# One of four block sums per pair moved from a DMA add to a VectorE add, in a product made of seven block products

## The chip, the cores and the metric

The kernel runs on one core of a Trainium2 chip. The metric is the device time of one execution in microseconds (us). The median of three executions of the kernel before is 2121.72 us. The engines are named as the profile names them: PE is TensorE (matmuls), DVE is VectorE, ACT is ScalarE, POOL is GpSimd and SP is SyncE; POOL and SP here mostly issue DMAs.

## The reference, cut to what matters

Two transformer blocks run on 512 tokens of width 1024, in float32. The part that the change touches is the second feed-forward layer (SwiGLU) of the first block:

```python
def swiglu(x, w_gu, w_down):
    g, u = jnp.split(x @ w_gu, 2, axis=-1)
    return (jax.nn.silu(g) * u) @ w_down

u = modulate(rmsnorm(h, norm3_g[l]), mod[:, 2, 0], mod[:, 2, 1])
h = h + FFN_RES_WEIGHT * mod[:, 2, 2][:, None, :] * swiglu(u, ffn2_w_gu[l], ffn2_w_down[l])
```

`w_gu` is 1024 x 5632: 2816 gate columns and as many up columns.

## The kernel before

Every float32 matmul is made of three: each operand is split into a high part (ACT copies it to a rounded type, line 131 for weights, tile `whi`) and a low part (DVE subtracts the high part from the operand, line 132, tile `wlo`), and PE adds high x high, high x low and low x high.

The layer's 22 blocks of 128 gate columns (and their 22 up columns) are taken two at a time, so 11 pairs. Pairs 1 and 2 are computed plainly (`eight_pair`). The other nine (`seven_pair`) use a product with seven block products where the plain way takes eight: the pair's weights and the tokens form a 2 x 2 block matrix each, and sums of blocks are multiplied. Here `w11` and `w12` are the upper and lower 512 rows of the pair's 256 gate columns, `w21` and `w22` those of its up columns. Each block is a tile of 128 partitions x 1024 float32 (512 KB).

The weight sums of a pair are made in `Seven.run`, all four by DMAs that POOL issues and that add into their target (`add`, line 584): `s1 += w22`, `w21 += w11`, `s1 += w11`, `s1 += w12`, where `s1` is loaded with the same data as `w21`. The tile `s1` is therefore used three times, each time with one more summand: the product called q5 here takes it after the first sum, q6 after the second of its sums, q3 after the third. A sum may only be added when the split before it has read `s1`, and the next split waits for the sum. In the trace the tiles `w11`, `w21` and `s1` are all named `w_sum`, and `w12` and `w22` lie in a tile `w_raw`: a DMA `w_sum<-w_sum` is `w21 += w11` or `s1 += w11`, a DMA `w_sum<-w_raw` is `s1 += w22` or `s1 += w12`.

The order on the engines comes from the scheduler, which follows the program as far as data allow. ACT, and DVE behind it, split a pair's seven weights in the order q5, q7 (`w21`), p1 (`w11`), q6, p2 (`w12`), q4 (`w22`), q3, and a split may use a buffer (four of them) only when PE has done with the product four splits earlier: q6 follows the q3 of the pair before, p2 the own q5, q4 the own q7, q3 the own p1. Each product is 24 matmuls of 256 columns. On PE they stand in the order q5, q7, p1, q6, the first 10 matmuls of q4, p2, the other 14 of q4, q3. The product p2 is accumulated on the bank `ca` of p1, so it must wait until ACT has copied p1's result out (line 588); this copy stands on ACT behind the high part of q3's split. Engines and queues take their instructions strictly in order.

The pairs and the down projections (`down_tiles`, lines 162 to 164 with `m_hi` and `m_lo`) alternate: two pairs by seven products, down; three, down; three, down; one, down. "First", "second" and "third" pair below are places in such a group; the group of three that starts at 904.55 us serves as the example. POOL's queue also holds `w21 += w11` of pairs that are still to come. The loads (line 562) are issued by SP, from a ring of six `w_sum` tiles and two `w_raw` tiles.

Of the kernel before, what the change touches and what calls it, by code (L numbers as in the profile page):

```python
# [25 lines left out]
def kernel(  # L26
# [7 lines left out]
    nc = tc.nc  # L34
# [13 lines left out]
    def z_bank(shape=(P, S)):  # L48
        return ps.tile(list(shape), F32, tag="z", name="z_ps")
# [32 lines left out]
    with tc.tile_pool(name="stage", bufs=1) as stage:  # L82
# [41 lines left out]
        def split_w(src, hi=None, lo=None):  # L124
            if hi is None:
                shape = [P, src.shape[1], src.shape[2]]
                hi, lo = (
                    wp.tile([P, 8 * P], F32R, tag=tag, name=tag, bufs=4)[
                        :, 0:shape[1] * shape[2]].rearrange("p (k n) -> p k n", n=shape[2])
                    for tag in ("whi", "wlo"))  # L130
            nc.scalar.activation(out=hi, in_=src, func=AF.Copy)  # L131
            nc.vector.tensor_tensor(out=lo, in0=src, in1=hi.bitcast(F32), op=ALU.subtract)  # L132
            return hi, lo
# [271 lines left out]
        for half in range(2):  # L405
# [4 lines left out]
            for kind in range(2):  # L410
                c0 = kind * D + 512 * half
                pr = z_bank()
                for kk in range(2):
                    wa = stage.tile([P, 4, 512], F32, tag="wa", name="wa", bufs=4)
                    nc.sync.dma_start(
                        out=wa, in_=w_ada[0][512 * kk:512 * (kk + 1), c0:c0 + 512].rearrange(
                            "(k p) n -> p k n", p=P))
# [82 lines left out]
    class Seven:  # L500
# [76 lines left out]
        def run(self, weights, upper, lower):  # L577

            w11, w12, w21, w22, s1 = weights

            def add(to, of):
                nc.gpsimd.dma_start(out=to, in_=of, accum_op=ALU.add)

            def copy(acc):
                v = self.ev()
                nc.scalar.activation(out=v, in_=acc, func=AF.Copy)  # L588
                return v

            add(s1, w22)
            add(w21, w11)
            q5 = split_w(s1)
            add(s1, w11)
            cc = z_bank()
            self.times(cc, q5, self.diff(0), True)
            v5 = copy(cc)
            q7 = split_w(w21)
            cd = z_bank()
            self.times(cd, q7, self.diff(2), True)  # L600
            v7 = copy(cd)
            p1 = split_w(w11)
            ca = z_bank()
            self.times(ca, p1, self.plain(0, H1), True)
            v1 = copy(ca)
            q6 = split_w(s1)
            add(s1, w12)
            cb = z_bank()
            self.times(cb, q6, self.diff(1), True)
            nc.vector.tensor_add(out=v1, in0=v1, in1=cb)  # L610
            p2 = split_w(w12)
            self.times(ca, p2, self.plain(HK, H1), False)
            upper(ca, 0)
            nc.vector.tensor_add(out=v5, in0=v5, in1=v1)
            nc.vector.tensor_sub(out=v7, in0=v7, in1=v5)
            q4 = split_w(w22)
            self.times(cd, q4, self.diff(3), False)
            q3 = split_w(s1)
            self.times(cc, q3, self.plain(HK, H2), False)
            nc.vector.tensor_add(out=v5, in0=cc, in1=v1)  # L620
            upper(v5, 1)
            lower(v7, 1)
            nc.vector.tensor_sub(out=v1, in0=cd, in1=v1)
            lower(v1, 0)
# [112 lines left out]
    with ExitStack() as mx:  # L737
# [140 lines left out]
        with tc.tile_pool(name="mrg", bufs=2) as gp:  # L878
# [28 lines left out]
            for j, cols, w in down_tiles(w_out[0], KT):  # L907
                pd = mm_bank()[:, 0:cols.stop - cols.start]
                with behind(nxt, j, cols):
                    proj(pd, w, mg, cols=cols)  # L910
                nc.vector.scalar_tensor_tensor(out=h[j][:, cols], in0=pd, scalar=gate(1, j),
                                               in1=h[j][:, cols], op0=ALU.mult, op1=ALU.add)
# [7 lines left out]
        out=wfg[:, :, 0:16], in_=wi[:, O_F:O_F + 16].rearrange("(k p) n -> p k n", p=P)))  # L920
# [30 lines left out]
    with ExitStack() as mx:  # L951
        with ExitStack() as ax:
# [5 lines left out]
            with tc.tile_pool(name="att2", bufs=2) as ap:  # L958
# [81 lines left out]
                for j in range(KT):  # L1040
                    nc.vector.scalar_tensor_tensor(out=h[j], in0=h[j], scalar=g_fin[:, j:j + 1],
                                                   in1=pb, op0=ALU.mult, op1=ALU.mult)
# [164 lines left out]
            for m in range(NB):  # L1207
# [5 lines left out]
                for q in range(2):  # L1213
# [5 lines left out]
                                        in1=mhalf[:, 0:1], op=ALU.pow)  # L1219
# [21 lines left out]
        with ExitStack() as gx:  # L1241
            agp = gx.enter_context(tc.tile_pool(name="ga2", bufs=8))
            av = []
            with tc.tile_pool(name="gm2", bufs=2) as gp:
# [4 lines left out]
                for q in range(4):  # L1249
                    w = by_feature(load_w(wi[:, 256 * q:256 * (q + 1)], KT, 256))  # L1250
                    for r in range(2):
# [7 lines left out]
                        for n in range(NB):  # L1259
# [4 lines left out]
                                             in1=bsb[:, g:g + 1, :].to_broadcast([P, NB, P]))  # L1264
                        nc.vector.tensor_mul(out=zu, in0=zu,
                                             in1=mixed.rearrange("p n t -> p (n t)"))
# [46 lines left out]
    with tc.tile_pool(name="ffnb", bufs=2) as fp:  # L1313
        wu = w_up_2[0]
        for pi, (f0, f1) in enumerate(parts):
            ms = []
            for f in range(f0, f1):
# [4 lines left out]
                for br in range(2):  # L1322
# [10 lines left out]
                    for k in (1, 2):  # L1333
                        nc.vector.scalar_tensor_tensor(
                            out=y, in0=xp[:, k:k + S],
# [17 lines left out]
    with tc.tile_pool(name="fin", bufs=2) as fp:  # L1353
# [4 lines left out]
            out=gfb, in_=norm_final_g_2.rearrange("(o n) -> o n", o=1).to_broadcast([P, D]))  # L1358
# [3 lines left out]
        for q in range(4):  # L1362
            cs = slice(256 * q, 256 * (q + 1))
            w = by_row(load_w(w_ple_gate_2[0][:, cs], KT, 256), KT, 256)
            for m in range(NB):
# [24 lines left out]
                if q < 3:  # L1390
# [3 lines left out]
                                               in1=sums[:, m:m + 1], op0=ALU.mult, op1=ALU.add)  # L1394
# [66 lines left out]
```

## Time and profile before

| what | value |
|---|---|
| median of 3 executions | 2121.72 us (2117.65 to 2121.92) |
| the profiled execution, its own time | 2116.4 us |
| its span, first to last instruction | 2114.7 us |
| PE busy | 98% |
| DVE busy | 59% |
| ACT busy | 42% |
| POOL busy | 6% |
| the nine pairs by seven products | 831.6 to 1119.9 us |

The busy shares tell which engine has no room (PE), not what a single stage waits for. For that one reads the stage: where PE stops, what ended each stop, and what that engine had waited for in its turn. A row of the timeline gives the start, the duration, the engine, the line, the operation and its tiles, and in brackets how long the engine had been idle before it and what ended that. A matmul's duration overlaps its neighbours', so the pace of PE is read from start to start.

### The profile page before, as it was taken

To read this page: it belongs to the slowest core of one execution; us is meant where nothing else is said; L and a number is where in the kernel's file an instruction comes from. 1 tells how busy PE (TensorE), PEld (TensorE's weight loads), DVE (VectorE), ACT (ScalarE), POOL (GpSimd) and SP (SyncE) were. 2 spreads that over 40 slices of the span, in tenths; PEclk is the share of its full clock that TensorE was granted. 3 is DMA by queue.
4 is the path that set the end of the run, shared out by engine and by line. 5 is a ranking of instruction groups with operands and counts; after the bars stand their busy time and mean duration, and the time that the engine had idled before them with its cause. 6 is when DMAs were issued, how large, how long until landed. Compare 5 with 4: busy or idle time off the path is not lost.

```text
span 2114.7 us, 26551 instructions
## 1 busy us (share of the span) xinstructions
PE 2075.0 (98%) x10450; PEld 1715.8 (81%) x10450; DVE 1240.5 (59%) x2096; ACT 877.8 (42%) x1366; POOL 125.3 (6%) x192
## 2 busy tenths in 40 slices
PE   7999999999999999999999999999999999999998
PEld 5778888888778888998988876667888888888888
DVE  3775655466653356555657586746554566474665
ACT  4322222357653245333435454645233343242444
POOL 1000000000000000110100011102200000000000
PEclk9999999999999999999999999999999999999999
DMA  9766554331222356776643422213323332333332
GB/s 348 225 217 178 180 178 126 94 100 60 60 81 83 104 146 151 175 177 173 163 112 103 110 80 80 80 50 100 120 80 100 100 100 82 99 99 100 90 128 72
DMA packets 293792, 259.42 MB, mean 123 GB/s; under 512 B 7605, under 2 KB 276090, under 8 KB 293412
## 3 DMA queue, kind: packets, MB, share of 16 engines
q1 hardware_dynamic: 285136, 228.68, 35.4%
q0 software_dynamic: 7840, 27.96, 6.2%
q8 instruction: 82, 1.34, 0.3%
q10 hardware_dynamic: 692, 1.09, 0.1%
q14 instruction: 42, 0.34, 0.1%
HBM read 234.60 MB, written 4.23 MB: 113 GB/s over the span
## 4 chain that ended last, share of the span: by engine, by line
PE 48%; DVE 1%; issue 1%; ACT 1%; DMA 0%; POOL 0%; POOLq 0%; ACTq 0%; DVEq 0%
PE mm_ps L162 12%; PE mm_ps L164 12%; PE mm_ps L163 12%; PE mm_ps L175 2%; PE mm_ps L174 2%; PE mm_ps L176 2%; PE po_ps L1145 2%; PE z_ps L1138 1%; PE z_ps L1099 1%; PE z_ps L1101 1%; PE z_ps L541 0%; PE z_ps L548 0%; PE z_ps L546 0%; PE z_ps L1260 0%; DMA w_sum<-w_raw 0%
## 5 line engine op out<-in xcount | busy, mean ns | idle before, releaser
L131 ACT ACTIVATE whi<-w_raw 128x1024 fp32r<-128x1024 f32 (+2 forms) x340 | 347.1, 1024 | 718.5 <-PE mm_ps L163 552.2
L162 PE MATMUL mm_ps<-uh,whi 128*128 128x512 f32 (+1 forms) x1392 | 541.2, 391 | 5.2 <-ACT uh L307 2.0
L163 PE MATMUL mm_ps<-ul,whi 128*128 128x512 f32 x1392 | 542.1, 390 | 0.0
L164 PE MATMUL mm_ps<-uh,wlo 128*128 128x512 f32 x1392 | 541.5, 389 | 0.0
L132 DVE TENSOR_TENSOR wlo<-w_raw,whi 128x1024 fp32r<-128x1024 f32 (+2 forms) x340 | 408.7, 1204 | 168.5 <-ACT whi L131 164.9
L162 PEld LDWEIGHTS mm_ps<-uh,whi 128*128 128x128 f32 x1392 | 261.7, 189 | 61.2 <-ACT uh L307 3.2
L164 PEld LDWEIGHTS mm_ps<-uh,wlo 128*128 128x128 f32 x1392 | 262.6, 189 | 53.6 <-issue 1.6
L163 PEld LDWEIGHTS mm_ps<-ul,whi 128*128 128x128 f32 x1392 | 262.7, 189 | 52.5 <-issue 0.8
L164 PE MATMUL mm_ps<-m_hi,wlo 128*128 128x512 f32 (+1 forms) x560 | 211.6, 378 | 0.0
L162 PE MATMUL mm_ps<-m_hi,whi 128*128 128x512 f32 (+1 forms) x560 | 211.0, 379 | 0.4 <-DVE h L715 0.4
L163 PE MATMUL mm_ps<-m_lo,whi 128*128 128x512 f32 (+1 forms) x560 | 211.1, 377 | 0.0
L162 PEld LDWEIGHTS mm_ps<-m_hi,whi 128*128 128x128 f32 x560 | 105.2, 188 | 20.5 <-issue 0.8
L163 PEld LDWEIGHTS mm_ps<-m_lo,whi 128*128 128x128 f32 x560 | 105.3, 188 | 20.4 <-issue 0.4
L164 PEld LDWEIGHTS mm_ps<-m_hi,wlo 128*128 128x128 f32 x560 | 105.2, 188 | 20.1
L174 PE MATMUL mm_ps<-whi,uh 128*128 128x512 f32 (+1 forms) x288 | 99.9, 350 | 3.7 <-ACT whi L131 1.6
L175 PE MATMUL mm_ps<-wlo,uh 128*128 128x512 f32 (+1 forms) x288 | 98.8, 344 | 0.8 <-DVE wlo L132 0.8
L176 PE MATMUL mm_ps<-whi,ul 128*128 128x512 f32 (+1 forms) x288 | 97.5, 343 | 0.0
L131 ACT ACTIVATE whi<-w_sum 128x1024 fp32r<-128x1024 f32 x45 | 47.7, 1059 | 118.8 <-PE mm_ps L163 40.9
L132 DVE TENSOR_TENSOR wlo<-w_sum,whi 128x1024 fp32r<-128x1024 f32 x45 | 55.1, 1225 | 58.5 <-ACT whi L131 57.1
L200 DVE SCALAR_TENSOR_TENSOR ada_acc<-ada_w,csil,ada_acc 128x256 f32<-128x256 f32 x196 | 87.3, 481 | 1.9
L548 PE MATMUL z_ps<-uth,wlo 128*128 128x256 f32 x288 | 82.0, 285 | 3.1 <-DVE wlo L132 3.1
L541 PE MATMUL z_ps<-uth,whi 128*128 128x256 f32 x288 | 81.8, 284 | 0.5 <-ACT ev L588 0.4
(355 smaller groups left out, 3154.5 us busy)
## 6 DMA issues: line engine op xcount, KB each, us to landing
w_raw<-in_ffn_w_gu_dram SPq DMA_DIRECT2D x70, 512.0 KB, 5.3
ada_w<-in_w_ada_dram SPq DMA_DIRECT2D x28, 1024.0 KB, 5.2
w_raw<-in_w_up_dram SPq DMA_DIRECT2D x44, 512.0 KB, 4.2
w_raw<-in_w_in_dram SPq DMA_DIRECT2D x20, 1024.0 KB, 5.2
w_sum<-in_ffn_w_gu_dram SPq DMA_DIRECT2D x27, 512.0 KB, 4.4
w_raw<-in_ffn_w_down_dram SPq DMA_DIRECT2D x16, 768.0 KB, 4.5
w_raw<-in_w_mix_in_dram SPq DMA_DIRECT2D x24, 512.0 KB, 5.2
w_sum<-w_sum POOLq DMA_DIRECT2D x18, 512.0 KB, 6.8
```

The source lines that it names most:

```text
L131: nc.scalar.activation(out=hi, in_=src, func=AF.Copy)
L132: nc.vector.tensor_tensor(out=lo, in0=src, in1=hi.bitcast(F32), op=ALU.subtract)
L162: nc.tensor.matmul(acc, lhsT=a, rhs=uhi[:, cols], start=k == 0, stop=False)
L163: nc.tensor.matmul(acc, lhsT=a, rhs=ulo[:, cols], start=False, stop=False)
L164: nc.tensor.matmul(acc, lhsT=b, rhs=uhi[:, cols], start=False, stop=k == n - 1)
L174: nc.tensor.matmul(acc, lhsT=a, rhs=wh, start=k == 0, stop=False)
L175: nc.tensor.matmul(acc, lhsT=a, rhs=wl, start=False, stop=False)
L176: nc.tensor.matmul(acc, lhsT=b, rhs=wh, start=False, stop=k == kt - 1)
L200: nc.vector.scalar_tensor_tensor(out=acc[:, q, :], in0=v[:, k, :], scalar=csil[:, k:k + 1], in1=acc[:, q, :], op0=ALU.mult, op1=ALU.add)
L541: i = nc.tensor.matmul(a, lhsT=whi[:, k, rows], rhs=uhi, start=start and first is None, stop=False, skip_group_check=True)
L548: nc.tensor.matmul(a, lhsT=wlo[:, k, rows], rhs=uhi, start=False, stop=last, skip_group_check=True)
L1145: nc.tensor.matmul(po[64 * hd:64 * hd + 64, b * P:S], lhsT=vts[head // 4][:, b, c0:c0 + 64], rhs=pT, start=b == 0, stop=b == NB - 1, skip_ ...
```

## The change

One of the two sums that follow one another on `s1`, the addition of `w11` between q5 and q6, is made by a DVE instruction on the two tiles. The other three sums of each pair stay DMAs.

```diff
             add(s1, w22)
             add(w21, w11)
             q5 = split_w(s1)
-            add(s1, w11)
+            nc.vector.tensor_add(out=s1, in0=s1, in1=w11)
             cc = z_bank()
             self.times(cc, q5, self.diff(0), True)
```

POOL's queue at the second and third pair of the example group and the first of the next (`w_sum_7380`, `_7378`, `_7379` are `s1`, `w11` and `w21` of the second pair, `_7615`, `_7613`, `_7614` of the third, `_8049` and `_8048` `w21` and `w11` of the next group's first):

```order
 L584 DMA w_sum_7615<-w_raw_7616 128x1024
 L584 DMA w_sum_7614<-w_sum_7613 128x1024
-L584 DMA w_sum_7380<-w_sum_7378 128x1024
 L584 DMA w_sum_7380<-w_raw_7381 128x1024
 L584 DMA w_sum_8049<-w_sum_8048 128x1024
-L584 DMA w_sum_7615<-w_sum_7613 128x1024
 L584 DMA w_sum_7615<-w_raw_7616 128x1024
 L584 DMA w_sum_8284<-w_sum_8283 128x1024
```

The two sums with `w11` are gone; the other DMAs keep their order, `w21 += w11` of a later pair ahead of `s1 += w12` of the running one among them.

DVE at the same third pair (line 615 belongs to the pair before; `wlo_7625`, `wlo_7657` and `wlo_7688` are the low parts of q5, q7 and p1):

```order
 L132 TENSOR_TENSOR wlo_7625<-w_sum_7615,whi_7624 128x1024
 L615 TENSOR_TENSOR ev_7450<-ev_7450,ev_7419 128x512
+L594 TENSOR_TENSOR w_sum_7615<-w_sum_7615,w_sum_7613 128x1024
 L132 TENSOR_TENSOR wlo_7657<-w_sum_7614,whi_7656 128x1024
 L132 TENSOR_TENSOR wlo_7688<-w_sum_7613,whi_7687 128x1024
```

The sum stands two places behind the low part of q5 and directly ahead of that of q7. It stands so in every second and third pair; in the first pair of a group of three it comes directly behind q5's low part and ahead of an instruction of line 715 (down projection into `h`). On PE, ACT and SP no instruction changes its place.

## Rows read from the trace of the kernel before

**Rows 1.** The page: the span, and the engines' busy time, share and instructions.
```profile
span 2114.7 us, 26551 instructions
...
PE 2075.0 (98%) x10450; PEld 1715.8 (81%) x10450; DVE 1240.5 (59%) x2096; ACT 877.8 (42%) x1366; POOL 125.3 (6%) x192
```

**Rows 2.** Waits of PE, 780 to 1130 us: total us, times, longest.
```profile
PE z_ps L548 <- DVE wlo L132: 3.1, 4, 0.9
PE z_ps L541 <- ACT ev L588: 2.7, 5, 0.6
```

**Rows 3.** Timeline of PE: first matmuls of pairs, the matmul behind them, two stops.
```profile
904.55 0.28 PE L541 MATMUL z_ps<-uth,whi 128*128 128x256 f32 x1
...
924.70 0.28 PE L541 MATMUL z_ps<-uth,whi 128*128 128x256 f32 x1
...
937.82 0.39 PE L548 MATMUL z_ps<-uth,wlo 128*128 128x256 f32 x1 [0.88 <-DVE wlo L132]
...
939.61 0.39 PE L541 MATMUL z_ps<-uh,whi 128*128 128x256 f32 x1 [0.56 <-ACT ev L588]
...
947.14 0.28 PE L541 MATMUL z_ps<-uth,whi 128*128 128x256 f32 x1
...
971.17 0.40 PE L162 MATMUL mm_ps<-m_hi,whi 128*128 128x512 f32 x1
...
1023.99 0.28 PE L541 MATMUL z_ps<-uth,whi 128*128 128x256 f32 x1
...
1045.20 0.28 PE L541 MATMUL z_ps<-uth,whi 128*128 128x256 f32 x1
...
1067.04 0.40 PE L162 MATMUL mm_ps<-m_hi,whi 128*128 128x512 f32 x1
```

**Rows 4.** Timeline of ACT in the second pair: high parts p1, q6, q4, q3; copy.
```profile
921.90 1.06 ACT L131 ACTIVATE whi<-w_sum 128x1024 fp32r<-128x1024 f32 x1
930.77 1.06 ACT L131 ACTIVATE whi<-w_sum 128x1024 fp32r<-128x1024 f32 x1 [7.81 <-DMA w_sum<-w_sum]
...
934.87 1.04 ACT L131 ACTIVATE whi<-w_raw 128x1024 fp32r<-128x1024 f32 x1
...
938.01 1.06 ACT L131 ACTIVATE whi<-w_sum 128x1024 fp32r<-128x1024 f32 x1 [1.62 <-DMA w_sum<-w_raw]
938.98 0.58 ACT L588 ACTIVATE ev<-z_ps 128x512 f32<-128x512 f32 x1
```

**Rows 5.** Timeline of POOL in the second and third pair.
```profile
921.30 1.77 POOL L584 DMA_DIRECT2D w_sum<-w_sum  x2 [3.06 <-DMA w_sum<-in_ffn_w_gu_dram]
933.38 0.87 POOL L584 DMA_DIRECT2D w_sum<-w_raw  x1 [10.32 <-DVE wlo L132]
945.17 1.77 POOL L584 DMA_DIRECT2D w_sum<-w_sum  x2 [10.92 <-DVE wlo L132]
```

**Rows 6.** Timeline of DVE: a line 715, then the second and third pair.
```profile
896.59 0.75 DVE L715 SCALAR_TENSOR_TENSOR h<-mm_ps,gate,h 128x512 f32<-128x512 f32 x1 [1.99 <-PE mm_ps L164]
...
921.31 1.23 DVE L132 TENSOR_TENSOR wlo<-w_sum,whi 128x1024 fp32r<-128x1024 f32 x1 [1.46 <-ACT whi L131]
...
931.86 1.23 DVE L132 TENSOR_TENSOR wlo<-w_sum,whi 128x1024 fp32r<-128x1024 f32 x1 [5.54 <-ACT whi L131]
933.01 1.29 DVE L694 TENSOR_TENSOR ev<-ev 128x512 f32<-128x512 f32 x2
...
943.76 1.22 DVE L132 TENSOR_TENSOR wlo<-w_sum,whi 128x1024 fp32r<-128x1024 f32 x1 [0.36 <-ACT whi L131]
```

**Rows 7.** All of lines 132 (ns: min, median, max) and 584 (us).
```profile
L132 DVE TENSOR_TENSOR wlo<-w_raw,whi x340: 681/1224/3368, 8.8 to 2081.8; 128x1024 fp32r<-128x1024 f32 x146, 128x768 fp32r<-128x768 f32 x20, 128x512 fp32r<-128x512 f32 x4
L132 DVE TENSOR_TENSOR wlo<-w_sum,whi x45: 1218/1226/1227, 823.3 to 1109.5; 128x1024 fp32r<-128x1024 f32 x45
...
DMA to landing us min/median/max: 4.5/5.1/9.6
```

**Rows 8.** Timeline of SP: the loads of the third pair's `s1` and `w11`.
```profile
898.71 4.45 SPq L562 DMA_DIRECT2D w_sum<-in_ffn_w_gu_dram  x2
```

## The prediction, made before the changed kernel was run

> **What bounds the kernel now.** I read the page first: PE is busy 98% of 2114.7 us [rows 1], so only a stretch in which PE stops can give time back. Next came the list of what PE waits for while the pairs run: two causes belong to the seven products, low parts of weights that come late from DVE (3.1 us) and a copy on ACT (2.7 us) [rows 2]. These idle times understate the loss, because PE also loses pace around a stop, so I measured whole pairs from start to start [rows 3]. The example group's first pair takes 924.70 - 904.55 = 20.15 us, the pace of a product of 24 matmuls being 20.15 / 7 = 2.88 us. The second takes 947.14 - 924.70 = 22.44, the third 971.17 - 947.14 = 24.03. In the next group the second takes 1045.20 - 1023.99 = 21.21 and the third 1067.04 - 1045.20 = 21.84. Against 20.15 that is 2.29 + 3.88 + 1.06 + 1.69 = **8.92 us of stops**, all in second and third pairs of the two groups of three.
>
> Last I followed one stop back. In the second pair PE stops at 937.82 us for the low part of q4, and at 939.61 for the copy that must precede p2 [rows 3]. On ACT, q4's high part was made at 934.87 and the copy at 938.98, both late because ACT stood 7.81 us, until 930.77, in front of q6's high part, waiting for a DMA `w_sum<-w_sum` [rows 4]: it is `s1 += w11`. POOL had issued that DMA late and in company, directly behind the `w21 += w11` of the next pair, which had to wait for its own load until 921.30 [rows 5]. So the chain is: a POOL queue whose first entry waits for a load, two DMA sums at once, q6, everything behind q6 on ACT, PE. In the third pair the same two-fold issue stands at 945.17 [rows 5].
>
> **What is removed: the wait in front of q6.** Without the DMA, q6's high part needs ACT free (921.90 + 1.06 = 922.96, rows 4) and its buffer, which PE gives back with the end of the pair before, 924.70 [rows 3]. So it can run at 924.7 and not at 930.77, 6.1 us earlier. Its low part ends after 1.06 and 1.23 us and about 0.1 between, at 927.1 [rows 4, 7].
>
> What is late next, step by step on the second pair:
> - p2's buffer comes free with q5, 924.70 + 2.88 = 927.6, and q4's with q7, 930.5. q4's low part then ends at about 932.9. PE wants it after four products, at 936.2, so there are 3.3 us to spare.
> - `s1 += w12` stays a DMA. POOL can issue it 0.3 us behind q6's low part (as at 933.38, where that part, from 931.86, ended at 933.09; rows 5, 6), so at 927.4. From issue to the split that uses it there were 938.01 - 933.38 = 4.63 us [rows 4, 5], which gives 932.0. The split of q3 can't start before its buffer is free with p1, at 924.70 + 3 x 2.88 = 933.3. The DMA is no longer waited for.
> - The copy then ends at 933.4 + 1.06 + 0.58 = 935.0. PE wants p2 after q6 and 10 matmuls of q4, at 924.70 + 4 x 2.88 + 1.2 = 937.4: 2.4 us to spare. This is the thinnest cover. With the longest landing of line 584, 9.6 us [rows 7], the DMA would be there at 937.0, the copy done at 938.7 and PE stopped for 1.3 us.
>
> The third pair, which would start 2.29 us earlier, has the same distances. The price of this part is therefore between -8.92 us (all stops go) and, where the last-named stop remains, some microseconds less; I take -8.92, because the usual landing is the row of this very DMA and not the longest of 36.
>
> **What is added: nine DVE sums.** The trace has no sum of two float32 tiles of this size that writes float32; the nearest rows are the 45 low parts of the same tiles, 1.218 to 1.227 us, and the far end is the longest of line 132, 3.368 us [rows 7]. I take 1.23: 11 us of DVE in all. They lie beside PE as long as nobody on PE waits for what is queued behind. Queued behind are the low parts of q7 and p1. In the second pair DVE idles 1.46 us right there, ahead of 921.31, so the sum fits but for a trifle. In the third the idle time is 0.36 us ahead of 943.76 [rows 6], so q7's low part moves back by 0.8 to 0.9 us, to end near 945.9 if ACT is where it was. PE wants q7 one product into the pair, 947.14 + 2.88 = 950.0 in the old trace and 947.7 in the shifted one: 1.8 us left, more if ACT moves forward too. With 3.368 us in place of 1.23 this would turn into a stop of 0.3 us. In the first pairs the sum stands ahead of line 715, where DVE idles 1.99 us for PE [rows 6]. Over the whole span DVE is busy 59% [rows 1]. The sum waits for nothing new: q5's split has already waited for `s1 += w22`, and `w11` has long been loaded (third pair: issued from 898.71 [rows 8], used near 943). I cost it at nothing, with an upper end of 0.3 us for each of the two third pairs.
>
> **What is moved.** POOL loses nine of 36 issues and nothing overtakes. `w21 += w11` of a later pair still stands ahead of `s1 += w12`. For the third pair that entry is issued at 945.17 [rows 5], once its load is there; that load follows the release of the second pair's raw weights, which comes earlier by the 6 us that q6 gains. Nine DMAs of 512 KB fewer share the DMA engines; I count no gain for that.
>
> One rule speaks against a DVE sum beside POOL's DMAs. POOL's issue at 933.38 ran beside the two-input DVE instructions at 933.01 and kept its 0.87 us [rows 5, 6]. The Trainium skill (SBUF — State Buffer, "SBUF: two separate sides") says that DVE and GpSimd share a port pair under an exclusive lock, taken by a DVE instruction with two SBUF inputs against a GpSimd instruction that reads SBUF, and it tells of a software-issued DMA going from about 620 to 3100 ns beside certain DVE instructions. If the sums did this to the issue of `s1 += w12`, its landing would come some 2.5 us later by that page and eat the cover of p2, which is rival A with a larger chance; the trace shows no such lengthening for instructions of the same kind.
>
> **The sum.** Profiled execution: 2114.7 - 8.92 = 2105.8 us of span, or 2116.4 - 8.92 = 2107.5 us. The median of the runs shown is 5.3 us above the profiled execution, so **2121.72 - 8.92 = 2112.8 us** as a median.
>
> **Rivals.**
> - A. The DMA sum that stays, `s1 += w12`, becomes the last. Then the stops in front of p2 remain. For: in all four bad pairs PE has such a stop, and ACT still waited 1.62 us for this DMA [rows 4]. Against: that wait started late only because q6 did. The four stops with the lost pace around them are about 0.8 us each, 3.3 us; gain 5.6, time 2116.1.
> - B. POOL's queue stays the bound in third pairs: `w21 += w11` of the next group waits for its load and holds `s1 += w12` behind it. It decides if that load lands more than 2.4 us behind the low part of the third q6 (near 947.3). For: POOL stood so until 945.17 in the old trace [rows 5]. Against: the load starts earlier now. Third pairs would keep 3.88 + 1.69; gain 3.35, time 2118.4.
> - C. Slower: DVE takes over a wait that POOL had. If `w11` is not there when the sum's turn comes, DVE stands with all low parts behind it. It decides from about 2 to 5 us, the cover of q7. With a wait like ACT's 7.81 [rows 4] each of the five second and third pairs of the three groups would stop for some 4 us: 20 - 8.9 = 11 us slower, 2132.8. Against: the load is issued some 40 us ahead [rows 8].
> - D. The stops pass to something that no row shows, and nothing is won: 2121.7. That the sum stays a DMA is excluded by the order on POOL and DVE.
>
> **How the numbers follow.** Forecast 0.74, A 0.10, B 0.08, C 0.03, D 0.05. The three executions shown differ by 4.3 us, and about 0.2% (4.2 us) is what a measurement of this kernel can tell from no change. Faster by more than that are the forecast, save for a bad draw, and most of A: 0.82. Within it are B, D and the rest of A: 0.14. Slower: 0.04. The range takes the forecast with the profiled execution's level at its lower end, 2107.5, and reaches over A to about B, 2118.
>
> **What would show it.** After the change the second and third pairs should take 20.2 us each from first matmul to first matmul. ACT should no longer wait for `w_sum<-w_sum` in front of q6, and the waits of PE in lines 541 and 548 should be gone. DVE should show nine instructions of line 594 of about 1.23 us. A is shown by PE stops at line 541 behind the copy; B by a late POOL issue in third pairs only; C by idle time of DVE ahead of line 594 that a load ends. I am wrong if the pairs run at 20.2 us and the time hasn't moved: then a later stage has eaten the gain.

## The result and the profile after the change

The changed kernel takes **2108.57 us** (median of four executions, 2108.18 to 2109.99), the kernel before in the same comparison 2120.01 us (four, 2117.65 to 2121.92). The ratio is 0.9948 with a 95% interval of 0.9931 to 0.9965, so 7.4 to 14.6 us were won. The forecast was a gain of 8.92 us (a ratio of 0.9958) and 2112.8 us. A second comparison (five executions against fifteen) gave 2109.21 us against 2118.87 and a ratio of 0.9956 [0.9942, 0.9969], which is 9.3 us.

The page of the profiled execution, which itself took 2108.77 us; it answers to [rows 1]:

```profile
span 2107.0 us, 26536 instructions
...
PE 2074.2 (98%) x10450; PEld 1717.8 (82%) x10450; DVE 1250.9 (59%) x2105; ACT 878.3 (42%) x1366; POOL 115.3 (5%) x183
```

DVE has nine instructions more and POOL nine fewer; no share tells why the span is 7.7 us shorter. The waits of PE between 780 and 1130 us, all that are left (total us, times, longest):

```profile
PE mm_ps L162 <- ACT ev L671: 2.2, 2, 1.6
PE mm_ps L162 <- ACT uh L633: 1.3, 1, 1.3
PE z_ps L291 <- DVE acc L283: 0.4, 1, 0.4
```

The two rows on lines 541 and 548 [rows 2] are gone. The first matmuls of the second and third pairs of both groups of three, and the matmul behind each group, on PE's timeline [rows 3]:

```profile
926.30 0.28 PE L541 MATMUL z_ps<-uth,whi 128*128 128x256 f32 x1
...
946.46 0.28 PE L541 MATMUL z_ps<-uth,whi 128*128 128x256 f32 x1
...
966.62 0.40 PE L162 MATMUL mm_ps<-m_hi,whi 128*128 128x512 f32 x1
...
1019.44 0.28 PE L541 MATMUL z_ps<-uth,whi 128*128 128x256 f32 x1
...
1039.60 0.28 PE L541 MATMUL z_ps<-uth,whi 128*128 128x256 f32 x1
...
1059.76 0.40 PE L162 MATMUL mm_ps<-m_hi,whi 128*128 128x512 f32 x1
```

Each pair now takes 20.16 us, the late ones too, where they took 22.44, 24.03, 21.21 and 21.84. All nine pairs with their down projections ran from 833.16 to 1112.58 us, 279.42 us, against 288.29 us before (831.57 to 1119.86): 8.87 us less. The stage in one row (length, busy us and count of each engine, granted clock, DMA share, GB/s):

```profile
830.00:1120.00 290.00, 290.00 (x1992) 271.06 (x1991) 178.86 (x206) 120.43 (x154) 20.03 (x23) 1.00 0.56 145
```

PE has no idle time left there. What stood in front of q6 is seen on ACT, in the second pair [rows 4]: the high parts of q6, q4 and q3, then the copy.

```profile
926.43 1.06 ACT L131 ACTIVATE whi<-w_sum 128x1024 fp32r<-128x1024 f32 x1 [1.87 <-PE z_ps L546]
...
932.19 1.06 ACT L131 ACTIVATE whi<-w_raw 128x1024 fp32r<-128x1024 f32 x1 [0.29 <-ACT m_hi L651]
...
935.85 1.06 ACT L131 ACTIVATE whi<-w_sum 128x1024 fp32r<-128x1024 f32 x1 [2.12 <-DMA w_sum<-w_raw]
936.81 0.58 ACT L588 ACTIVATE ev<-z_ps 128x512 f32<-128x512 f32 x1
```

q6 is split 0.13 us after the pair's first matmul (926.30), and it was the buffer that PE gave back that released it. Before, it came 6.07 us after that point. q3 still waited for its DMA, 2.12 us. Over 800 to 1120 us ACT waited for the sums made by DMA as follows, in the kernel before and then after:

```profile
ACT whi L131 <- DMA w_sum<-w_sum: 36.2, 5, 9.4
ACT whi L131 <- DMA w_sum<-w_raw: 18.3, 6, 10.3
```

```profile
ACT whi L131 <- DMA w_sum<-w_raw: 5.9, 3, 2.1
```

POOL in the second and third pair [rows 5]: the two-fold issues are gone, and `s1 += w12` goes out right behind q6's low part (which begins at 927.83, in the DVE rows below).

```profile
923.17 0.88 POOL L584 DMA_DIRECT2D w_sum<-w_sum  x1 [3.41 <-DMA w_sum<-in_ffn_w_gu_dram]
929.34 0.87 POOL L584 DMA_DIRECT2D w_sum<-w_raw  x1 [5.29 <-DVE wlo L132]
943.33 0.87 POOL L584 DMA_DIRECT2D w_sum<-w_sum  x1 [13.11 <-DMA w_sum<-in_ffn_w_gu_dram]
949.50 0.87 POOL L584 DMA_DIRECT2D w_sum<-w_raw  x1 [5.30 <-DVE wlo L132]
```

DVE in the second pair [rows 6]: the new sum, q7's low part, q6's low part. Then all nine sums (ns, minimum, median, maximum).

```profile
921.00 1.22 DVE L594 TENSOR_TENSOR w_sum<-w_sum 128x1024 f32<-128x1024 f32 x1
922.91 1.23 DVE L132 TENSOR_TENSOR wlo<-w_sum,whi 128x1024 fp32r<-128x1024 f32 x1 [0.69 <-ACT whi L131]
...
927.83 1.22 DVE L132 TENSOR_TENSOR wlo<-w_sum,whi 128x1024 fp32r<-128x1024 f32 x1
```

```profile
L594 DVE TENSOR_TENSOR w_sum<-w_sum x9: 1219/1220/1228, 824.9 to 1082.5; 128x1024 f32<-128x1024 f32 x9
```

No sum had to wait for data, and q7's low part behind it came after ACT anyway, with 0.69 us to spare.

Why the span fell by 7.7 us and not by 8.87: the pairs began 1.59 us later in this execution, and what follows them was 0.4 us shorter. The later start is already there at 100 us: the copy of line 131 that begins at 100.06 us before begins at 101.87 us after, and at 99.19 us in the second profile of the changed kernel. It goes with the first 75 us, where the granted clock is at its half level (1.2 GHz) for a while in each execution. The stretch from 30 to 75 us before, after, and in the second profile of the changed kernel (the clock is the third number from the end):

```profile
30.00:75.00 45.00, 38.60 (x196) 28.44 (x196) 31.72 (x58) 16.53 (x23) 0.00 (x0) 0.96 0.89 292
```

```profile
30.00:75.00 45.00, 39.23 (x186) 29.06 (x185) 30.42 (x55) 16.23 (x23) 0.00 (x0) 0.89 0.87 284
```

```profile
30.00:75.00 45.00, 39.62 (x202) 29.25 (x199) 32.54 (x59) 16.61 (x24) 0.00 (x0) 0.96 0.92 300
```

In the last of these three the pairs start at 830.45 us, end at 1109.86 (279.41 us again), and the span is 2104.3 us. So the start of the pairs differs between executions of one kernel; the length of the pairs' stage doesn't, and that is what the experiments below are read by. "Stage" means this length.

### The profile page after: what moved, and what is told of

Its sections match the earlier page's. It is cut to its first block, busy times and chain, and to the rows that moved or that the text cites. A ratio compares the mean times of both kernels' runs of the same rounds, so it can differ in the third digit from the quotient of the medians.

```text
span 2107.0 us, 26536 instructions
## 1 busy us (share of the span) xinstructions
PE 2074.2 (98%) x10450; PEld 1717.8 (82%) x10450; DVE 1250.9 (59%) x2105; ACT 878.3 (42%) x1366; POOL 115.3 (5%) x183
## 4 chain that ended last, share of the span: by engine, by line
PE 95%; DVE 2%; ACT 1%; DMA 1%; SPq 1%; issue 1%; POOL 0%; POOLq 0%; ACTq 0%; DVEq 0%
PE mm_ps L162 24%; PE mm_ps L164 24%; PE mm_ps L163 24%; PE z_ps L548 3%; PE z_ps L546 3%; PE z_ps L541 3%; PE mm_ps L174 2%; PE mm_ps L175 2%; PE mm_ps L176 2%; PE po_ps L1145 2%; PE z_ps L822 1%; PE z_ps L1138 1%; PE z_ps L1099 1%; PE po_ps L833 1%; PE z_ps L1101 1%
## 5 line engine op out<-in xcount | busy, mean ns | idle before, releaser
L164 PEld LDWEIGHTS mm_ps<-uh,wlo 128*128 128x128 f32 x1392 | 262.8, 189 | 53.5 <-issue 1.6
L546 PE MATMUL z_ps<-utl,whi 128*128 128x256 f32 x288 | 81.5, 283 | 0.0
```

Source lines behind the costliest of these rows:

```text
L164: nc.tensor.matmul(acc, lhsT=b, rhs=uhi[:, cols], start=False, stop=k == n - 1)
L546: nc.tensor.matmul(a, lhsT=whi[:, k, rows], rhs=ulo, start=False, stop=False, skip_group_check=True)
```

## The experiments

The theory is that of the prediction: the sum `s1 += w11` came late because of where it stood in POOL's queue, this held q6 and all that is behind it on ACT, and PE stopped in the second and third pairs. Its rivals: the DMA as such is too slow, wherever it stands; it is the traffic of nine DMAs more; the gain comes from elsewhere in the nine pairs. Ratios are to the kernel before in the same comparison, with 95% intervals. Diffs are against the changed kernel.

**Second and third pairs only, and the other five only.**

```diff
-            nc.vector.tensor_add(out=s1, in0=s1, in1=w11)
+            if on_dve:
+                nc.vector.tensor_add(out=s1, in0=s1, in1=w11)
+            else:
+                add(s1, w11)
...
-                seven.run(weights, upper, lower)
+                seven.run(weights, upper, lower, f0 in (10, 12, 16, 18))
```

> The DVE sum only in the four second and third pairs of the groups of three; the other five pairs keep the DMA. My theory (PE stopped because q6's split in these four pairs waited for the DMA): all of the gain, every pair 20.2 us from first matmul to first matmul, time 0.4 to 0.55% under the kernel before. Rival (every DMA sum removed gives its share, by less traffic and less work on POOL): 4/9 of the gain, about 0.2%.

Measured: 2109.43 us, 0.9957 [0.9941, 0.9974]; all nine pairs take 20.15 or 20.16 us. The four sums of the late pairs give the whole gain. The other kernel has `f0 in (4, 6, 8, 14, 20)`:

> The complement: the DVE sum only in the first pairs, the second pair of the first group and the last pair; the four late pairs keep the DMA. My theory: no gain, the late pairs at 22.4, 24.0, 21.2 and 21.8 us within 0.5 us each, time within 0.1% of the kernel before. Rival (each sum gives its share): 5/9 of the gain, about 0.28% faster.

Measured: 2119.45 us, 1.0003 [0.9994, 1.0013]; the late pairs take 22.34, 23.79, 22.88 and 22.34 us, and PE's waits of the kernel before are back:

```profile
PE z_ps L548 <- DVE wlo L132: 4.3, 5, 0.9
PE z_ps L541 <- ACT ev L588: 3.1, 6, 0.6
```

Five sums on DVE in pairs that had no stop give nothing. One of the four late pairs missed its expectation: 22.88 us where 21.2 was expected to within 0.5. With it the late pairs lose 10.75 us here and not 8.9, so the size of the stops isn't fixed, though their place is. Where in the nine pairs the gain sits is settled by these two.

**The other sum on DVE.** `w21 += w11` is what stood ahead in the queue. If it goes to DVE, `s1 += w11` stays the DMA it was, with a clear way.

```diff
-            add(w21, w11)
+            nc.vector.tensor_add(out=w21, in0=w21, in1=w11)
             q5 = split_w(s1)
-            nc.vector.tensor_add(out=s1, in0=s1, in1=w11)
+            add(s1, w11)
```

> The other sum goes to DVE: w21 += w11 there, s1 += w11 a DMA as before, so as many DMAs as in the change. Theory that the queue made the wait (the DMA for q6 stood behind a w21 += w11 that waited for its load, and two sums ran at once): the DMA is issued about 0.3 us behind q5's low part, 5 us ahead of the pair's start, lands in 4.6 to 6.5 us, and at most 1.5 us of wait stays in front of q6; pairs 20.2 us, time as the changed kernel within 0.1%. Theory that the latency of a DMA between two uses of s1 is the cost, wherever it is queued: ACT still waits several us in front of q6, late pairs 21 us or more, at most half of the gain.

Measured: 2114.30 us, 0.9982 [0.9972, 0.9991]. The pairs say one thing and the total another. In the pairs the theory holds: all nine take 20.15 to 20.17 us, the stage 279.41 us. POOL, ACT and PE in the second pair (the sum's issue, q6's high part, the pair's first matmul):

```profile
922.63 0.87 POOL L584 DMA_DIRECT2D w_sum<-w_sum  x1 [1.07 <-DVE wlo L132]
```

```profile
929.10 1.06 ACT L131 ACTIVATE whi<-w_sum 128x1024 fp32r<-128x1024 f32 x1 [2.69 <-DVE ev L620]
```

```profile
928.15 0.28 PE L541 MATMUL z_ps<-uth,whi 128*128 128x256 f32 x1
```

The DMA is issued 5.5 us ahead of the pair's start, right when q5's low part is done, and q6 is split 0.95 us into the pair. No stop follows. So the DMA is fast enough when nothing that waits stands ahead of it, and "too slow as such" falls.

Yet the total, expected within 0.1% of the changed kernel, is 5.1 us (0.24%) above its 2109.2. In the profiled executions the loss stands in two places outside the stage. The first is ahead of the pairs. From the first `uh` (line 633) to the first pair's start it takes 835.02 - 781.5 = 53.5 us, in the changed kernel 833.16 - 782.2 = 51.0. Six of the nine sums on DVE wait for loads here, 5.1 us in all. The first does so ahead of the pairs, directly in front of a low part `ul` that PE needs, and PE stops for 0.93 us:

```profile
787.59 1.23 DVE L592 TENSOR_TENSOR w_sum<-w_sum 128x1024 f32<-128x1024 f32 x1 [1.43 <-DMA w_sum<-in_ffn_w_gu_dram]
```

```profile
789.20 0.39 PE L163 MATMUL mm_ps<-ul,whi 128*128 128x256 f32 x1 [0.93 <-DVE ul L636]
```

This is rival C on a small scale, for a sum that the change did not move; the one stop is 0.93 of the 2.5 us, and no row shown here accounts for the rest. The second place is far behind: from the end of the stage to the end of the span it takes 997.0 us, not 994.4. At 1440 us the scheduler has put matmuls in another order, PE stops for 1.88 us at line 174 where the changed kernel stops for 0.76 us, and the granted clock is down behind it:

```profile
1440.00:1444.00 4.00, 2.75 (x7) 2.17 (x8) 4.00 (x5) 2.45 (x5) 0.52 (x1) 0.58 0.17 49
```

The two places make 2.5 + 2.6 = 5.1 us. The two spans differ by 4.4 us, because this execution had reached the first `uh` 0.7 us earlier.

**The last sum on DVE instead.** `s1 += w11` is a DMA again, `s1 += w12` goes to DVE.

```diff
-            nc.vector.tensor_add(out=s1, in0=s1, in1=w11)
+            add(s1, w11)
...
-            add(s1, w12)
+            nc.vector.tensor_add(out=s1, in0=s1, in1=w12)
```

> The other way round: s1 += w12 on DVE, s1 += w11 a DMA as before. Theory (every late split stands behind q6 on ACT): q6 still waits 6 to 9 us, the stops for q4's low part stay (about 1 us in three of the late pairs), only those in front of p2 go (about 0.8 us each): half of the gain or less, 0.1 to 0.25% under the kernel before, late pairs 20.4 to 22.5 us. Rival (any sum taken from POOL's queue relieves it): late pairs at 20.2 us and all of the gain.

Measured: 2111.64 us, 0.9968 [0.9956, 0.9981]. In the groups of three the pairs take 20.15, 22.71, 20.16 and 20.15, 22.92, 20.16 us: second pairs keep their stop, third pairs lose it. POOL, then ACT at q6 of the second pair, then PE's stop in it:

```profile
924.37 1.77 POOL L584 DMA_DIRECT2D w_sum<-w_sum  x2 [3.27 <-DMA w_sum<-in_ffn_w_gu_dram]
945.84 0.87 POOL L584 DMA_DIRECT2D w_sum<-w_sum  x1 [19.70 <-DVE wlo L132]
948.72 0.87 POOL L584 DMA_DIRECT2D w_sum<-w_sum  x1 [2.00 <-DMA w_sum<-in_ffn_w_gu_dram]
```

```profile
933.82 1.06 ACT L131 ACTIVATE whi<-w_sum 128x1024 fp32r<-128x1024 f32 x1 [7.78 <-DMA w_sum<-w_sum]
```

```profile
942.01 0.38 PE L548 MATMUL z_ps<-uth,wlo 128*128 128x256 f32 x1 [2.01 <-DVE wlo L132]
```

In the second pair the two sums still go out together behind a load, and q6 waits 7.78 us, nearly the 7.81 of before. In the third the same DMA goes out alone at 945.84, q6 is split at 951.40, 0.9 us after the pair's first matmul, and there is no stop. It goes out alone because its place in the queue is another: `w21 += w11` of the next group, which stood ahead of it in the kernel before, goes out behind it here, at 948.72, when its load is there. So the company in the queue and the load ahead of it make the stop. The expectation missed this: its theory would have kept a stop in third pairs, with half of the gain or less (0.1 to 0.25%), and the total came out at 0.32%. By the pairs 2.56 + 2.77 = 5.3 of 8.9 us of stops stay, so 3.6 should be won; the total says 6.8 (4.0 to 9.3). The profiled execution is the slowest of the six (2115.49 us). What makes up the rest isn't settled.

**Both sums on DVE.** The changed kernel, and `s1 += w12` by `nc.vector.tensor_add` too.

> The last sum of the chain, s1 += w12, goes to DVE as well. The trace of the changed kernel has no stop of PE left in the pairs, so nothing is to be won: within 0.1% of the changed kernel, and ACT's 2.1 us of waiting in front of q3 gone. Rival (the remaining DMA still costs): up to 0.1% faster. Or DVE now waits for a load: slower, with idle time of DVE in front of the new sum.

Measured: 2107.05 us, 0.9944 [0.9931, 0.9956], with the changed kernel beside it at 0.9956 [0.9942, 0.9969]:

> The changed kernel once more, for a narrower interval. By whole pairs the gain is 8.9 us of some 2120, so a ratio of 0.9958; the first measurement had 0.9948 with 0.9931 to 0.9965. Expected 0.994 to 0.9965.

The intervals overlap, and the medians differ by 0.10%, which theory and rival both allowed; the total can't tell them apart. The pairs can: they take 20.15 or 20.16 us in both, although ACT no longer waits in front of q3 there. The DMA that stayed costs PE nothing, and rival A is excluded from both sides. This kernel isn't shown to be the better one.

**As many DMAs as before.** Each pair adds one block into a buffer in DRAM that nobody reads (it is filled from `h` once, ahead of the pairs), in one kernel in the place of the removed sum, in another at the pair's end.

```diff
             nc.vector.tensor_add(out=s1, in0=s1, in1=w11)
+            nc.gpsimd.dma_start(out=self.ghost, in_=w11, accum_op=ALU.add)
```

> The changed kernel with one more DMA per pair on POOL's queue, which adds w11 into a buffer in DRAM that nobody reads: the number of POOL's DMAs is that of the kernel before, only nobody waits for this one. Theory (the wait in front of q6 was the cost): time as the changed kernel within 0.15%, pairs 20.2 us. Rival (traffic and POOL's work were the cost): late pairs above 21 us again and half of the gain or more lost, 0.2 to 0.5%.

Measured: 2126.37 us, 1.0036 [1.0023, 1.0049], slower than before. It didn't measure traffic, since the scheduler put the added DMA of a later pair ahead of `s1 += w12`, and it waited for that pair's load:

```profile
937.64 0.87 POOL L598 DMA_DIRECT2D ghost<-w_sum  x1 [8.01 <-DMA w_sum<-in_ffn_w_gu_dram]
938.19 1.21 POOL L587 DMA_DIRECT2D w_sum<-w_raw  x1
```

In the changed kernel that sum went out 3.0 us after the pair's first matmul (929.34 - 926.30), here 7.1 us after it (938.19 - 931.05). PE's stops in front of p2 return, in the lines of this kernel:

```profile
PE z_ps L544 <- ACT ev L591: 12.9, 5, 4.2
```

The second pair of the first group takes 26.14 us, the late pairs up to 25.06. It is rival B's mechanism, brought about by the added entry: one DMA that waits for a load, at the head of POOL's queue, costs PE several us. With the added DMA at the end of the pair, behind `s1 += w12`, it stands in nobody's way:

```diff
             q3 = split_w(s1)
+            nc.gpsimd.dma_start(out=self.ghost, in_=s1, accum_op=ALU.add)
```

> The changed kernel with one more DMA per pair on POOL's queue, this time of s1 behind its last sum, so that it stands behind s1 += w12 in the queue and not ahead of it (in the first try the scheduler had put it ahead, with a wait for a later pair's load). It adds into a buffer in DRAM that nobody reads. POOL's issues and the bytes are those of the kernel before. Theory (the wait was the cost): within 0.15% of the changed kernel, pairs 20.2 us. Rival (traffic and POOL's work): late pairs above 21 us, 0.2% or more lost.

Measured: 2110.33 us, 0.9965 [0.9954, 0.9977]. Eight pairs take 20.15 or 20.16 us and one 20.61. POOL issues as many DMAs here as in the kernel before:

```profile
928.38 0.87 POOL L587 DMA_DIRECT2D w_sum<-w_raw  x1 [3.19 <-DVE wlo L132]
935.98 0.87 POOL L622 DMA_DIRECT2D ghost<-w_sum  x1 [6.72 <-DMA w_sum<-w_raw]
```

So neither the number of POOL's DMAs nor their bytes made the 8.9 us (though the added ones write to DRAM); of the stage 0.45 us is lost. Behind the stage the profiled execution lost 1.8 us more, with the granted clock down at 1438 us.

**How much cover DVE has.** Behind the sum, four or eight instructions that put the maximum of `s1` and `s1` into `s1`, each as long as the sum and of no effect on its value.

```diff
             nc.vector.tensor_add(out=s1, in0=s1, in1=w11)
+            for _ in range(4):
+                nc.vector.tensor_tensor(out=s1, in0=s1, in1=s1, op=ALU.max)
```

> The changed kernel with four more DVE instructions of the same size per pair on s1 (the maximum of s1 with itself, in place), 36 in all, 41 to 44 us of DVE time. Theory (DVE has about 5 us of cover ahead of q7 and 4 us ahead of q6 in the pairs): same time as the changed kernel within 0.15%, pairs 20.2 to 20.5 us. Rival (DVE work lies on the path there): up to 44 us, 2% slower.

Measured with four: 2114.82 us, 0.9981 [0.9972, 0.9990]. Thirty-six instructions of 1.22 us, 44 us of DVE, lengthen the stage by 3.2 us (to 282.6). The second and third pair of a group of three take 42.1 us together, where 20.5 each was the most expected, and the total is 0.27% above the changed kernel, where 0.15% was; of that, the stage has 0.15%. PE stops for a low part twice, both times in a third pair:

```profile
PE z_ps L548 <- DVE wlo L132: 1.5, 2, 0.8
```

Of the 5.6 us between this kernel and the changed one, 2.2 more lie behind the stage (996.6 us from its end to the span's end, not 994.4), where PE stops near 1440 us as with the other sum on DVE. With eight:

> Eight more per pair, 72 in all, 82 to 88 us. s1 is then ready for q6 some 9 us after the sum, about as late as by the DMA before. Theory (what counts is when s1 is ready for q6, and what stands behind on DVE): stops are back, second and third pairs 21 us or more, time 0.3 to 1.5% above the changed kernel. If it doesn't move, the cover is larger than I worked out and the wait in front of q6 was not the cause.

Measured: 2153.50 us, 1.0168 [1.0154, 1.0182], 2.1% above the changed kernel, so the stops are back and are larger than the 0.3 to 1.5% expected. DVE can't hold the eight, and PE stops for high parts of weights:

```profile
PE z_ps L541 <- ACT whi L131: 28.2, 6, 6.7
```

Four further instructions (4.9 us) thus use up the cover of third pairs, and eight (9.8 us) are too many for all. The sum of the change takes 1.22 us.

## Why the prediction was right, point by point

- **The size of the gain.** 8.92 us of stops were counted from pair to pair, and the stage is 8.87 us shorter. The sum of the waits [rows 2] alone would have said 5.8; the pairs, from first matmul to first matmul, gave the right number.
- **The chain.** POOL's queue, q6, ACT, PE: borne out by its two cures. Take either DMA of the two-fold issue out, `s1 += w11` (the change) or `w21 += w11`, and the second pairs run at 20.16 or 20.17 us; take out the DMA behind them, and they don't (22.71 and 22.92). Third pairs lost their stop by that last cure too, but there the queue's order had changed with it. In the second pair both parts of the chain counted. The low part of q5 ended at 919.25, so the sum could have gone out at about 919.5; the load ahead held it until 921.8. It landed 8.8 us later in company, where it took 6.4 us with `w21 += w11` on DVE and 5.5 us alone in the third pair above.
- **q6 at the pair's start.** Forecast 0.0 us after the pair's first matmul, measured 0.13.
- **q3's DMA, a step that failed.** "The DMA is no longer waited for" was wrong. From its issue to q3's split it took 935.85 - 929.34 = 6.5 us, not the 4.63 read from the row, and ACT waited 2.12 us for it; the split came 0.9 us later than 926.30 + 3 x 2.88 = 934.9, where its buffer was due. The copy ended at 937.4, and PE wanted p2 at 926.30 + 4 x 2.88 + 1.2 = 939.0. So the thinnest cover was 1.6 us and not 2.4. It held, and the term stayed zero, but one duration from one row was too little to size a cover with: this DMA landed 6.4 us after its issue, the one of that row 4.5. Why it took longer isn't shown; the landings of line 584 ran from 4.5 to 9.2 us after the change, about as before [rows 7].
- **The DVE sum.** Forecast 1.23 us each, measured 1.219 to 1.228; its cost to PE nothing. q7's low part ended at 924.1 in the second pair, 5.0 us before PE wanted it (926.30 + 2.88 = 929.2). In the third pair the forecast was 1.8 us of cover; there it began at 943.07, ended at 944.3, and was wanted at 946.46 + 2.88 = 949.3, so 5.0 us too, because ACT had moved forward with it.
- **The port rule.** The Trainium skill (SBUF — State Buffer, "SBUF: two separate sides") let one fear a longer issue on POOL beside the sums. Four issues began while a sum ran; each kept its 0.87 us, and they landed 4.5 to 5.5 us later (the median of line 584 was 5.2), so nothing of the sort shows here. One of them, on POOL and on DVE:

```profile
848.37 0.87 POOL L584 DMA_DIRECT2D w_sum<-w_sum  x1 [11.69 <-DVE ev L615]
```

```profile
848.02 1.22 DVE L594 TENSOR_TENSOR w_sum<-w_sum 128x1024 f32<-128x1024 f32 x1
```

- **The level.** The forecast for the median was 4.2 us above the result, that for the profiled execution (2107.5) 1.3 below it (2108.77). It took over the 5.3 us by which the median of three stood above the profiled execution, and this distance was a thing of the draw: with fifteen executions the kernel before has a median of 2118.87 (2115.50 to 2122.35). That the median lies only 1.1 us inside the range's lower end (2107.5) is therefore no proof of a good range: the 5.3 us were added to the forecast without a cause. The profiled execution of after lost 1.6 us by its start and gained 0.4 at the end, as told above.
- **The rivals.** A: no stop behind the copy in any of the nine pairs. B: not in the changed kernel; the added DMA showed that its mechanism is real. The row it was read from, POOL's issue at 945.17 [rows 5], names a low part on DVE and not the load as what ended the wait; after the change the row of that issue (943.33) names the load. C: not for this sum; for `w21 += w11` on DVE 2.5 us were lost ahead of the pairs, 0.93 of them in a stop that it made. D: the stops passed to nothing.

## What to carry to other kernels

When an engine waits for a DMA, look at what stood ahead of that DMA in its queue and what it was issued together with before calling the DMA slow; here taking either of two neighbours out of the queue cured the same stop. Size stops by comparing repetitions from start to start, since idle times alone left a third out here (5.8 of 8.9 us). Here a sum moved to a busier engine was free because its data were there long ago and the engine had some 5 us to spare in front of what PE wanted next; four further instructions used that up, and a sum on data still being loaded held what stood behind it.

## What the runs showed of the hardware that was not expected

- **Behind a stop the granted clock may fall, and the stop's length didn't decide it.** With the added DMA ahead in the queue, PE stopped for 1.92 us and the clock was at its half level (1.2 GHz) for a part of the stretch behind (a mean of 0.71); 78 us later it stopped for 3.30 us and the clock stayed at 1.00:

```profile
970.91 0.39 PE L544 MATMUL z_ps<-uh,whi 128*128 128x256 f32 x1 [1.92 <-ACT ev L591]
...
1048.93 0.39 PE L544 MATMUL z_ps<-uh,whi 128*128 128x256 f32 x1 [3.30 <-ACT ev L591]
```

```profile
970.00:975.00 5.00, 4.09 (x23) 4.09 (x24) 3.98 (x5) 1.59 (x3) 0.00 (x0) 0.71 0.83 264
1050.00:1055.00 5.00, 5.00 (x44) 5.00 (x43) 4.96 (x7) 2.61 (x3) 0.86 (x1) 1.00 0.54 181
```

  With eight further DVE instructions, whose stops went up to 6.7 us, the mean clock of 830 to 1120 us was 0.92. In the kernel before, with stops of 0.9 us at most in the pairs, this mean was 1.00, so its stops cost no clock.
- **The start differs from run to run.** At half clock for 3.4 or 10.2 us in the first 75 us (added up from the mean clock of stretches of 5 us), the same kernel reaches its pairs at 830.45 or 833.16 us: 2.7 us, nearly a third of the gain that was to be measured.
- **Time was lost far from the change.** Two kernels that differ from the changed one only in these nine pairs (`w21 += w11` on DVE, and four further instructions) lost 2.6 and 2.2 us at about 1440 us, some 320 us behind them, where the scheduler had ordered matmuls in another way and the clock fell. Two others lost time there in the order of the kernel before: with the DVE sum in the other five pairs, and with the added DMA at the pair's end, PE made the same two stops (1.6 and 0.75 us) as in the kernel before, and the clock fell behind them (means of 0.92 and 0.96 over 1420 to 1465 us, 1.00 in the kernels before and after the change). So the new order isn't needed for such a loss. In such a comparison the total doesn't say what the stage does; the stage's own length does.
